# Instance normalisation over 512 instances: tiles of 64 KiB per partition in three slots in place of 32 KiB in six, with the squares shared by two engines and the last slot in three pieces

## The chip, the cores and the metric

The kernel runs on one core of a Trainium2 chip; the other cores are idle. The metric is the device time of one execution in microseconds (us). A profile's span is about 1.7 us shorter than the timed value of the same execution.

A run is called fast or slow: slow when it is over 1.5% above the fastest of the same kernel. On one core this is only a label by time. Ratios are the mean time of one kernel's fast runs over that of the other's fast runs of the same rounds, so not quite the ratio of the medians that are quoted.

PE is TensorE, DVE is VectorE, ACT is ScalarE, SP the engine that issues the loads. "ACTq" and "SPq" lines of a profile are the issues of transfers by ACT and SP.

## The reference, cut to what matters

```python
x = randn(8, 64, 32, 64, 64)              # float32, 512 instances of 131,072 elements, 268 MB
mean = np.mean(x, axis=(2, 3, 4), keepdims=True)
var = np.var(x, axis=(2, 3, 4), keepdims=True)
return ((x - mean) / np.sqrt(var + eps)).astype(np.float32)
```

Every byte is read once and written once: 536.87 MB through the core's 16 DMA engines.

## The kernel before

An instance is spread over 16 partitions of 8,192 columns, so a tile holds 8 instances and there are 64 tiles. Six slots of 32 KiB per partition hold tiles that are loading, computing or storing.

```python
    SPLIT = 16
    IPT = P // SPLIT
    F = n_elem // SPLIT          # 8192
    SLOTS = 6
    # ... data_pool = tile_pool(name="data", bufs=SLOTS)
    def load(g):
        t = data_pool.tile([P, F], fp32, name="xt")
        nc.sync.dma_start(out=t, in_=x_t[g])
        return t

    def compute(t):
        cut = F // 2
        # DVE sums t[:, :cut], ACT sums t[:, cut:]  -> sums [P, 2]
        # PE: matmul with a block matrix of 1/n_elem -> mean on every partition; DVE: neg_mean
        nc.scalar.activation(
            out=unused, in_=t, func=Act.Square, bias=neg_mean, accum_out=squares
        )
        # PE: matmul -> variance; ACT: sqrt; DVE: reciprocal (scale), neg_mean * scale (bias)
        # DVE normalises t[:, cut:], ACT normalises t[:, :cut], both in place

    with tc.manual_schedule():
        for g in range(n_tiles):
            t = load(g)
            compute(t)
            nc.scalar.dma_start(out=out_t[g], in_=t)
```

Of the kernel before, what the change touches and what calls it, by code (L numbers as in the profile page):

```python
# [1 line left out]

# [4 lines left out]


@with_exitstack
def kernel(  # L10
    ctx: ExitStack,
    tc: tile.TileContext,
    x: bass.AP,
    eps: bass.AP,
    out: bass.AP,
):
    nc = tc.nc
    fp32 = mybir.dt.float32
    Alu = mybir.AluOpType
    Act = mybir.ActivationFunctionType  # L20

    P = 128
    B, C, D, H, W = x.shape
    n_inst = B * C
    n_elem = D * H * W
    eps_f = float(eps)

    SPLIT = 16
    IPT = P // SPLIT
    F = n_elem // SPLIT  # L30
    n_tiles = n_inst // IPT
    SLOTS = 6

    x_t = x.rearrange("b c d h w -> (b c) (d h w)").rearrange(
        "(k i) (s f) -> k (i s) f", i=IPT, s=SPLIT
    )
    out_t = out.rearrange("b c d h w -> (b c) (d h w)").rearrange(
        "(k i) (s f) -> k (i s) f", i=IPT, s=SPLIT
    )

    singles = ctx.enter_context(tc.tile_pool(name="singles", bufs=1))
    data_pool = ctx.enter_context(tc.tile_pool(name="data", bufs=SLOTS))
    stat_pool = ctx.enter_context(tc.tile_pool(name="stats", bufs=4))
    psum_pool = ctx.enter_context(
        tc.tile_pool(name="psum", bufs=2, space=bass.MemoryType.PSUM)
    )


    avg = singles.tile([P, P], fp32, name="avg")
    nc.vector.memset(avg, 1.0 / n_elem)  # L50
    nc.gpsimd.affine_select(  # L51
        out=avg,
        in_=avg,
        pattern=[[-SPLIT, IPT], [0, SPLIT]],
        compare_op=Alu.is_ge,
        fill=0.0,
        base=0,
        channel_multiplier=1,
    )
    nc.gpsimd.affine_select(  # L60
        out=avg,
        in_=avg,
        pattern=[[SPLIT, IPT], [0, SPLIT]],
        compare_op=Alu.is_ge,
        fill=0.0,
        base=SPLIT - 1,
        channel_multiplier=-1,
    )

    eps_t = singles.tile([P, 1], fp32, name="eps_t")  # L70
    nc.vector.memset(eps_t, eps_f)  # L71

    unused = singles.tile([P, F], mybir.dt.uint8, name="unused")

    def load(g):
        t = data_pool.tile([P, F], fp32, name="xt")
        nc.sync.dma_start(out=t, in_=x_t[g])
        return t

    def compute(t):  # L80
        cut = F // 2
        sums = stat_pool.tile([P, 2], fp32, name="sums")
        nc.vector.reduce_sum(  # L83
            out=sums[:, 0:1], in_=t[:, :cut], axis=mybir.AxisListType.X
        )
        nc.scalar.activation(  # L86
            out=unused[:, cut:],
            in_=t[:, cut:],
            func=Act.Identity,
            accum_out=sums[:, 1:2],  # L90
        )
        mean_ps = psum_pool.tile([P, 2], fp32, name="mean_ps")
        nc.tensor.matmul(out=mean_ps, lhsT=avg, rhs=sums, start=True, stop=True)  # L93
        neg_mean = stat_pool.tile([P, 1], fp32, name="neg_mean")
        nc.vector.tensor_reduce(  # L95
            out=neg_mean,
            in_=mean_ps,
            axis=mybir.AxisListType.X,
            op=Alu.add,
            negate=True,  # L100
        )
        squares = stat_pool.tile([P, 1], fp32, name="squares")
        nc.scalar.activation(  # L103
            out=unused, in_=t, func=Act.Square, bias=neg_mean, accum_out=squares
        )
        var_ps = psum_pool.tile([P, 1], fp32, name="var_ps")
        nc.tensor.matmul(out=var_ps, lhsT=avg, rhs=squares, start=True, stop=True)  # L107
        std = stat_pool.tile([P, 1], fp32, name="std")
        nc.scalar.activation(out=std, in_=var_ps, func=Act.Sqrt, bias=eps_t)  # L109
        scale = stat_pool.tile([P, 1], fp32, name="scale")  # L110
        nc.vector.reciprocal(out=scale, in_=std)  # L111
        bias = stat_pool.tile([P, 1], fp32, name="bias")
        nc.vector.tensor_mul(out=bias, in0=neg_mean, in1=scale)  # L113
        nc.vector.tensor_scalar(  # L114
            out=t[:, cut:],
            in0=t[:, cut:],
            scalar1=scale,
            scalar2=bias,
            op0=Alu.mult,
            op1=Alu.add,  # L120
        )
        nc.scalar.activation(  # L122
            out=t[:, :cut], in_=t[:, :cut], func=Act.Identity, scale=scale, bias=bias
        )


    with tc.manual_schedule():
        for g in range(n_tiles):
            t = load(g)
            compute(t)  # L130
            nc.scalar.dma_start(out=out_t[g], in_=t)  # L131


# [1 line left out]
_INS = ['x', 'eps']  # L135
_OUTS = [((8, 64, 32, 64, 64), 'float32')]

_NUMBERS = {'eps': 9.999999747378752e-06}


# [26 lines left out]
```

## Time and profile before

| what | value | view |
|---|---|---|
| time | 1249.34 us median of 3 (1249.26 to 1250.57) | timed runs |
| span | 1247.6 us | page |
| busy: ACT, DVE | 961.6 us (77%), 467.4 us (37%) | page, part 1 |
| DMA | 9 or more tenths in 39 of 40 slices, mean 430 GB/s | page, part 2 |
| a data packet | 32,768 bytes, median 1,213 ns | packet records of the trace |
| one tile: DMA, compute | 19.4 us (8.39 MB in and out at 432 GB/s), 17.5 us | windows, timeline |

The page of the kernel before; the PE line gives the busy time of each engine, in the DMA row a digit is the busy share of one fortieth of the span in tenths, and the queue lines give packets, megabytes and the share of the 16 engines' span:

```profile
span 1247.6 us, 1828 instructions
...
PE 73.6 (6%) x256; PEld 64.2 (5%) x256; DVE 467.4 (37%) x322; ACT 961.6 (77%) x386; POOL 0.9 (0%) x6
...
DMA  9999999999999999999999999999999999999998
GB/s 403 420 437 434 434 427 436 435 435 427 435 436 434 434 428 435 435 434 427 437 435 434 433 429 437 435 432 427 437 436 434 429 431 435 436 434 425 437 436 364
DMA packets 18443, 536.99 MB, mean 430 GB/s; under 512 B 2048, under 2 KB 2048, under 8 KB 2048
...
q1 hardware_dynamic: 9216, 268.44, 49.9%
q10 hardware_dynamic: 9216, 268.44, 49.8%
```

The two queues (q1 loads, q10 stores) together keep the engines busy for 99.7% of the span. What is not at the full rate are the first slice (the first packet comes late) and the last one. The end, in windows of 5 us (the last two columns are the DMA's busy share and its rate):

```profile
1225.00:1230.00 5.00, 0.59 (x2) 0.50 (x2) 1.02 (x3) 3.85 (x4) 0.00 (x0) 1.00 0.99 426
1230.00:1235.00 5.00, 0.00 (x0) 0.00 (x0) 1.71 (x1) 3.15 (x1) 0.00 (x0) 1.00 0.81 347
1235.00:1240.00 5.00, 0.00 (x0) 0.00 (x0) 0.00 (x0) 0.00 (x0) 0.00 (x0) 1.00 0.98 419
```

At 1230 to 1235 us the rate falls to 347 GB/s: the store before the last has drained while ACT and DVE still normalise the last tile.

### The profile page before, as it was taken

Reading aid. Unit: us, or ns where it says so; the run is one execution under the profiler, and the core shown is the slowest. Engines: PE = TensorE matmul, PEld = TensorE weight load, DVE = VectorE, ACT = ScalarE, POOL = GpSimd, SP = SyncE. Lnnn points to the kernel's source line nnn. Section 1 sums busy time; section 2 is a strip of 40 time slices with the busy share of each in tenths; the row PEclk is TensorE's granted clock in tenths of the full one; section 3 lists DMA queues with packets and bytes.
Section 4 is the critical chain, followed back from the end, with each engine's and each line's share of the span. In section 5 each row is a group of like instructions: output and inputs, shape, how many; then the busy total and the mean of one; then the engine's idle time right before and its main releaser. Section 6 shows DMA issues by size and latency. Waiting matters only on the chain.

```text
span 1247.6 us, 1828 instructions
## 1 busy us (share of the span) xinstructions
PE 73.6 (6%) x256; PEld 64.2 (5%) x256; DVE 467.4 (37%) x322; ACT 961.6 (77%) x386; POOL 0.9 (0%) x6
## 2 busy tenths in 40 slices
PE   0000000000000000000000000000000000000000
PEld 0000000000000000000000000000000000000000
DVE  2344433433334334343343433434334333343331
ACT  5888888787777877778777777777787777877774
POOL 0000000000000000000000000000000000000000
DMA  9999999999999999999999999999999999999998
GB/s 403 420 437 434 434 427 436 435 435 427 435 436 434 434 428 435 435 434 427 437 435 434 433 429 437 435 432 427 437 436 434 429 431 435 436 434 425 437 436 364
DMA packets 18443, 536.99 MB, mean 430 GB/s; under 512 B 2048, under 2 KB 2048, under 8 KB 2048
## 3 DMA queue, kind: packets, MB, share of 16 engines
q1 hardware_dynamic: 9216, 268.44, 49.9%
q10 hardware_dynamic: 9216, 268.44, 49.8%
q14 instruction: 9, 0.07, 0.0%
q8 instruction: 2, 0.03, 0.0%
HBM read 268.44 MB, written 268.44 MB: 430 GB/s over the span
## 4 chain that ended last, share of the span: by engine, by line
ACT 45%; DVE 32%; another core or an unknown queue 12%; PE 6%; issue 2%; DMA 1%; ACTq 0%
ACT unused L103 37%; DVE sums L83 19%; DVE xt L114 10%; ACT xt L122 4%; ACT unused L86 3%; PE var_ps L107 3%; PE mean_ps L93 3%; ACT std L109 1%; DMA xt<-in_x_dram 1%; DVE scale L111 1%; DVE neg_mean L95 1%; DVE bias L113 1%; ACTq L131 0%; ACT L109 0%
## 5 line engine op out<-in xcount | busy, mean ns | idle before, releaser
L103 ACT ACTIVATE unused<-xt,neg_mean 128x8192 uint8<-128x8192 f32 x64 | 455.8, 7121 | 100.6 <-DVE neg_mean L95 100.6
L83 DVE TENSOR_REDUCE sums<-xt 128x1 f32<-128x4096 f32 x64 | 282.8, 4419 | 167.6 <-DMA xt<-in_x_dram 167.6
L86 ACT ACTIVATE unused<-xt 128x4096 uint8<-128x4096 f32 x64 | 231.5, 3617 | 96.1 <-DMA xt<-in_x_dram 91.5
L122 ACT ACTIVATE xt<-xt,bias,scale 128x4096 f32<-128x4096 f32 x64 | 243.3, 3801 | 31.3 <-DVE bias L113 31.3
L111 DVE RECIPROCAL scale<-std 128x1 f32<-128x1 f32 x64 | 10.5, 164 | 530.8 <-ACT std L109 530.8
L114 DVE TENSOR_SCALAR xt<-xt,scale,bias 128x4096 f32<-128x4096 f32 x64 | 154.4, 2413 | 2.7 <-DVE bias L113 0.3
L93 PE MATMUL mean_ps<-sums,avg 128*128 128x2 f32 x128 | 36.0, 351 | 670.9 <-DVE sums L83 573.9
L93 PEld LDWEIGHTS mean_ps<-sums,avg 128*128 128x128 f32 x128 | 32.1, 311 | 674.7 <-ACT unused L86 657.1
L107 PE MATMUL var_ps<-squares,avg 128*128 128x1 f32 x128 | 37.6, 363 | 484.1 <-ACT unused L103 484.1
L107 PEld LDWEIGHTS var_ps<-squares,avg 128*128 128x128 f32 x128 | 32.1, 312 | 489.6 <-ACT unused L103 489.6
L109 ACT ACTIVATE std<-var_ps,eps_t 128x1 f32<-128x1 f32 x64 | 16.7, 261 | 42.7 <-PE var_ps L107 42.7
L95 DVE TENSOR_REDUCE neg_mean<-mean_ps 128x1 f32<-128x2 f32 x64 | 10.2, 160 | 60.1 <-PE mean_ps L93 60.1
L103 ACT ACTIVATION_READ_ACCUMULATOR unused<-xt,neg_mean 128x1 f32 x64 | 11.9, 187 | 0.0
L86 ACT ACTIVATION_READ_ACCUMULATOR unused<-xt 128x1 f32 x64 | 11.9, 186 | 0.0
L113 DVE TENSOR_TENSOR bias<-neg_mean,scale 128x1 f32<-128x1 f32 x64 | 10.2, 160 | 2.2
L86 ACT ACT_TABLE_LOAD x1 | 1.3, 1283 | 0.8 <-PEq L148 0.8
L109 ACT ACT_TABLE_LOAD x1 | 1.3, 1283 | 0.0
L50 DVE MEMSET avg<- 128x128 f32 x1 | 0.2, 165 | 0.9 <-PEq L148 0.9
L51 POOL TENSOR_SCALAR_AFFINE_SELECT avg<-avg 128x128 f32<-128x128 f32 x1 | 0.3, 343 | 0.6 <-DVE eps_t L71 0.6
L60 POOL TENSOR_SCALAR_AFFINE_SELECT avg<-avg 128x128 f32<-128x128 f32 x1 | 0.3, 338 | 0.1
L148 POOL MEMSET const-bfloat16-1.0<- 128x1 bf16 x1 | 0.1, 102 | 0.0
L148 POOL MEMSET const-uint8-127<- 128x1 uint8 x1 | 0.1, 102 | 0.0
(3 smaller groups left out, 0.3 us busy)
## 6 DMA issues: line engine op xcount, KB each, us to landing
xt<-in_x_dram SPq DMA_DIRECT2D x64, 4096.0 KB, 53.3
out_dram<-xt ACTq DMA_DIRECT2D x64, 4096.0 KB, 45.2
```

The source lines that it names most:

```text
L51: nc.gpsimd.affine_select(out=avg, in_=avg, pattern=[[-SPLIT, IPT], [0, SPLIT]], compare_op=Alu.is_ge, fill=0.0, base=0, channel_multiplier=1,
L83: nc.vector.reduce_sum(out=sums[:, 0:1], in_=t[:, :cut], axis=mybir.AxisListType.X)
L86: nc.scalar.activation(out=unused[:, cut:], in_=t[:, cut:], func=Act.Identity, accum_out=sums[:, 1:2],)
L93: nc.tensor.matmul(out=mean_ps, lhsT=avg, rhs=sums, start=True, stop=True)
L95: nc.vector.tensor_reduce(out=neg_mean, in_=mean_ps, axis=mybir.AxisListType.X, op=Alu.add, negate=True,)
L103: nc.scalar.activation(out=unused, in_=t, func=Act.Square, bias=neg_mean, accum_out=squares)
L107: nc.tensor.matmul(out=var_ps, lhsT=avg, rhs=squares, start=True, stop=True)
L109: nc.scalar.activation(out=std, in_=var_ps, func=Act.Sqrt, bias=eps_t)
L111: nc.vector.reciprocal(out=scale, in_=std)
L113: nc.vector.tensor_mul(out=bias, in0=neg_mean, in1=scale)
L114: nc.vector.tensor_scalar(out=t[:, cut:], in0=t[:, cut:], scalar1=scale, scalar2=bias, op0=Alu.mult, op1=Alu.add,)
L122: nc.scalar.activation(out=t[:, :cut], in_=t[:, :cut], func=Act.Identity, scale=scale, bias=bias)
```

## The change

Its intent: fewer and larger transfers (32 in place of 64 tiles), the compute of a tile shortened by giving DVE a share of the squares, and a short end, because the last slot is loaded, computed and stored as three pieces of 8, 4 and 4 instances. The share of DVE needs scratch, which goes to PSUM, and its columns stay centred in place. The mean matrix carries the minus sign. The core of the diff (the averaging matrices for three row splits and unchanged calls are cut):

```diff
-    SLOTS = 6
+    SLOTS = 3
+    COLS = 16384
+    BIG = P * COLS // n_elem                 # 16 instances
+    tail = [
+        (n_inst - BIG, BIG // 2),
+        (n_inst - BIG // 2, BIG // 4),
+        (n_inst - BIG // 4, BIG // 4),
+    ]
 ...
-        cut = F // 2
+        a = w * 29 // 64                     # DVE sums [:a], ACT sums [a:]
+        b = w * 3 // 16                      # DVE squares [:b], ACT squares [b:]
+        c = w * 39 // 64                     # DVE normalises [:c], ACT [c:]
 ...
         nc.scalar.activation(
-            out=unused, in_=t, func=Act.Square, bias=neg_mean, accum_out=squares
-        )
+            out=of_act[:, : w - b], in_=t[:, b:], func=Act.Square,
+            bias=neg_mean, accum_out=squares[:, 1:2],
+        )
+        nc.vector.tensor_scalar(
+            out=t[:, :b], in0=t[:, :b], scalar1=neg_mean, scalar2=None, op0=Alu.add
+        )
+        nc.vector.tensor_tensor_reduce(
+            out=of_dve[:, :b], in0=t[:, :b], in1=t[:, :b], scale=1.0, scalar=0.0,
+            op0=Alu.mult, op1=Alu.add, accum_out=squares[:, 0:1],
+        )
 ...
-        for g in range(n_tiles):
-            t = load(g)
-            compute(t)
-            nc.scalar.dma_start(out=out_t[g], in_=t)
+        for g in range(n_big):
+            load(whole(g), *groups[g])
+            compute(tiles[g], groups[g][1])
+            store(tiles[g], *groups[g])
+        last = list(pieces(whole(n_big)))
+        for t, first, n in last:
+            load(t, first, n)
+        for t, first, n in last:
+            compute(t, n)
+            store(t, first, n)
```

Loads on SP and stores on ACT: the kernel before had this already.

More of the change, by code (lines that the diff above doesn't have):

```diff
@@ L26 @@
     eps_f = float(eps)
-    SPLIT = 16
-    IPT = P // SPLIT
-    F = n_elem // SPLIT
-    n_tiles = n_inst // IPT
-    SLOTS = 6
-    x_t = x.rearrange("b c d h w -> (b c) (d h w)").rearrange(
-        "(k i) (s f) -> k (i s) f", i=IPT, s=SPLIT
-    )
-    out_t = out.rearrange("b c d h w -> (b c) (d h w)").rearrange(
-        "(k i) (s f) -> k (i s) f", i=IPT, s=SPLIT
-    )
+    SLOTS = 3
+    COLS = 16384
+    x_f = x.rearrange("b c d h w -> (b c) (d h w)")
+    out_f = out.rearrange("b c d h w -> (b c) (d h w)")
@@ L41 @@
+    BIG = P * COLS // n_elem
+    groups = [(i, BIG) for i in range(0, n_inst - BIG, BIG)]
+    n_big = len(groups)
+    tail = [
[3 more added lines that the diff above has]
+    ]
     singles = ctx.enter_context(tc.tile_pool(name="singles", bufs=1))
     data_pool = ctx.enter_context(tc.tile_pool(name="data", bufs=SLOTS))
-    stat_pool = ctx.enter_context(tc.tile_pool(name="stats", bufs=4))
+    stat_pool = ctx.enter_context(tc.tile_pool(name="stats", bufs=3))
@@ L44 @@
+    psum_one = ctx.enter_context(
+        tc.tile_pool(name="psum_one", bufs=1, space=bass.MemoryType.PSUM)
+    )
     psum_pool = ctx.enter_context(
-        tc.tile_pool(name="psum", bufs=2, space=bass.MemoryType.PSUM)
+        tc.tile_pool(name="psum", bufs=1, space=bass.MemoryType.PSUM)
     )
-    avg = singles.tile([P, P], fp32, name="avg")
-    nc.vector.memset(avg, 1.0 / n_elem)
-    nc.gpsimd.affine_select(
-        out=avg,
-        in_=avg,
-        pattern=[[-SPLIT, IPT], [0, SPLIT]],
-        compare_op=Alu.is_ge,
-        fill=0.0,
-        base=0,
-        channel_multiplier=1,
-    )
@@ L60, with averaging @@
-    nc.gpsimd.affine_select(
-        out=avg,
-        in_=avg,
-        pattern=[[SPLIT, IPT], [0, SPLIT]],
-        compare_op=Alu.is_ge,
-        fill=0.0,
-        base=SPLIT - 1,
-        channel_multiplier=-1,
-    )
+    def averaging(split):
+        neg = singles.tile([P, P], fp32, name=f"neg{split}")
+        nc.vector.memset(neg, -1.0 / n_elem)
+        nc.gpsimd.affine_select(
+            out=neg,
+            in_=neg,
+            pattern=[[-split, P // split], [0, split]],
+            compare_op=Alu.is_ge,
+            fill=0.0,
+            base=0,
+            channel_multiplier=1,
+        )
+        nc.gpsimd.affine_select(
+            out=neg,
+            in_=neg,
+            pattern=[[split, P // split], [0, split]],
+            compare_op=Alu.is_ge,
+            fill=0.0,
+            base=split - 1,
+            channel_multiplier=-1,
+        )
+        return neg
@@ L70 @@
+    negs = {n: averaging(P // n) for n in sorted({n for _, n in groups + tail})}
     eps_t = singles.tile([P, 1], fp32, name="eps_t")
     nc.vector.memset(eps_t, eps_f)
-    unused = singles.tile([P, F], mybir.dt.uint8, name="unused")
-    def load(g):
-        t = data_pool.tile([P, F], fp32, name="xt")
-        nc.sync.dma_start(out=t, in_=x_t[g])
-        return t
-    def compute(t):
-        cut = F // 2
+    of_act = singles.tile([P, COLS - COLS * 3 // 16], mybir.dt.uint8, name="of_act")
@@ L82, in compute, with rows, load @@
+    of_dve = psum_one.tile([P, COLS * 3 // 16], fp32, name="of_dve")
+    def rows(ap, first, n):
+        return ap[first : first + n].rearrange("i (s f) -> (i s) f", s=P // n)
+    def load(t, first, n):
+        nc.sync.dma_start(out=t, in_=rows(x_f, first, n))
+    def compute(t, n):
+        w = t.shape[1]
+        a = w * 29 // 64
+        b = w * 3 // 16
+        c = w * 39 // 64
+        neg = negs[n]
         sums = stat_pool.tile([P, 2], fp32, name="sums")
         nc.vector.reduce_sum(
-            out=sums[:, 0:1], in_=t[:, :cut], axis=mybir.AxisListType.X
+            out=sums[:, 0:1], in_=t[:, :a], axis=mybir.AxisListType.X
@@ L85, in compute @@
         )
         nc.scalar.activation(
-            out=unused[:, cut:],
-            in_=t[:, cut:],
+            out=of_act[:, : w - a],
+            in_=t[:, a:],
             func=Act.Identity,
@@ L91, in compute @@
         )
-        mean_ps = psum_pool.tile([P, 2], fp32, name="mean_ps")
-        nc.tensor.matmul(out=mean_ps, lhsT=avg, rhs=sums, start=True, stop=True)
+        halves = psum_pool.tile([P, 2], fp32, name="halves")
+        nc.tensor.matmul(out=halves, lhsT=neg, rhs=sums, start=True, stop=True)
         neg_mean = stat_pool.tile([P, 1], fp32, name="neg_mean")
-        nc.vector.tensor_reduce(
-            out=neg_mean,
-            in_=mean_ps,
-            axis=mybir.AxisListType.X,
-            op=Alu.add,
-            negate=True,
-        )
-        squares = stat_pool.tile([P, 1], fp32, name="squares")
+        nc.vector.reduce_sum(out=neg_mean, in_=halves, axis=mybir.AxisListType.X)
+        squares = stat_pool.tile([P, 2], fp32, name="squares")
+        nc.scalar.activation(
+            out=of_act[:, : w - b],
+            in_=t[:, b:],
+            func=Act.Square,
+            bias=neg_mean,
+            accum_out=squares[:, 1:2],
+        )
+        nc.vector.tensor_scalar(
+            out=t[:, :b],
+            in0=t[:, :b],
+            scalar1=neg_mean,
+            scalar2=None,
+            op0=Alu.add,
+        )
+        nc.vector.tensor_tensor_reduce(
+            out=of_dve[:, :b],
+            in0=t[:, :b],
+            in1=t[:, :b],
+            scale=1.0,
+            scalar=0.0,
+            op0=Alu.mult,
+            op1=Alu.add,
+            accum_out=squares[:, 0:1],
+        )
+        neg_var = psum_pool.tile([P, 1], fp32, name="neg_var")
+        nc.tensor.matmul(
+            out=neg_var, lhsT=neg, rhs=squares[:, 0:1], start=True, stop=False
+        )
+        nc.tensor.matmul(
+            out=neg_var, lhsT=neg, rhs=squares[:, 1:2], start=False, stop=True
+        )
+        std = stat_pool.tile([P, 1], fp32, name="std")
         nc.scalar.activation(
-            out=unused, in_=t, func=Act.Square, bias=neg_mean, accum_out=squares
+            out=std, in_=neg_var, func=Act.Sqrt, scale=-1.0, bias=eps_t
         )
-        var_ps = psum_pool.tile([P, 1], fp32, name="var_ps")
-        nc.tensor.matmul(out=var_ps, lhsT=avg, rhs=squares, start=True, stop=True)
-        std = stat_pool.tile([P, 1], fp32, name="std")
-        nc.scalar.activation(out=std, in_=var_ps, func=Act.Sqrt, bias=eps_t)
         scale = stat_pool.tile([P, 1], fp32, name="scale")
@@ L113, in compute @@
         nc.vector.tensor_mul(out=bias, in0=neg_mean, in1=scale)
+        nc.scalar.activation(
+            out=t[:, c:], in_=t[:, c:], func=Act.Identity, scale=scale, bias=bias
+        )
         nc.vector.tensor_scalar(
-            out=t[:, cut:],
-            in0=t[:, cut:],
+            out=t[:, b:c],
+            in0=t[:, b:c],
             scalar1=scale,
@@ L121, in compute, with whole, pieces, store @@
         )
-        nc.scalar.activation(
-            out=t[:, :cut], in_=t[:, :cut], func=Act.Identity, scale=scale, bias=bias
-        )
-    with tc.manual_schedule():
-        for g in range(n_tiles):
-            t = load(g)
-            compute(t)
-            nc.scalar.dma_start(out=out_t[g], in_=t)
+        nc.vector.tensor_scalar(
+            out=t[:, :b], in0=t[:, :b], scalar1=scale, scalar2=None, op0=Alu.mult
+        )
+    tiles = {}
+    def whole(g):
+        tiles[g] = data_pool.tile([P, COLS], fp32, name="xt")
+        return tiles[g]
+    def pieces(t):
+        at = 0
+        for first, n in tail:
+            width = n * n_elem // P
+            yield t[:, at : at + width], first, n
+            at += width
+    def store(t, first, n):
+        nc.scalar.dma_start(out=rows(out_f, first, n), in_=t)
+    with tc.manual_schedule():
+        for g in range(n_big):
[8 more added lines that the diff above has]
+            store(t, first, n)
 _INS = ['x', 'eps']
```

## The prediction

> **What bounds it now.** The 16 DMA engines. The page's DMA row is 9 in 39 of 40 slices, and the queue table gives 49.9% + 49.8% = 99.7% of the engines' span; 536.99 MB moved at a mean 430 GB/s. The trace's own packet records show how: 16,384 data packets of 32,768 bytes, nearly all taking 1,213 ns, plus 2,048 completion writes of 4 bytes at 9 ns. Per engine that is 1,024 x 1.213 + 128 x 0.009 = 1,243.3 us of the 1,247.6 us span. 32,768 B / 1.213 us x 16 = 432 GB/s, and the steady windows read 432. The Trainium skill (DMA: Bandwidth & Descriptors, "Where 436 GB/s comes from") puts the ceiling at 435.2 GB/s; the trace is 0.7% under it. ACT (77% busy) and DVE (37%) wait for data: DVE's first reduction waits 167.6 us in all for loads.
>
> **What is left to win.** About 1.2 us before the first packet, about 1.3 us at 1,232-1,234 us where the store before last has drained and the last tile is still being normalised, and some 3 us from the last full-rate stretch to the end (stragglers, completion).
>
> **What the change does.**
> 1. Bytes: the same 536.87 MB. Queues as before. No gain.
> 2. Rows of 64 KiB, 32 + 32 big transfers for 64 + 64: completion writes fall by about 0.6 us per engine. If a row becomes one 64 KiB packet, and if the 8 ns of 1,213 above the ceiling's 1,205 is a cost per packet, another 512 x 8 ns = 4 us go; if it is a cost per byte, or rows are cut into 32 KiB, nothing. I count half: -2 us.
> 3. Compute per 16,384-column tile, estimated from the trace's durations (ACT 0.86 ns per column plus 0.3 us, DVE sum 1.04, in-place scale 0.55-0.59): sums 8.0, mean 1.0, squares 11.7 (ACT; DVE's share about 5), variance to scale 1.4, normalise 5.9: 28.5 us, against 2 x 17.5 = 35 us now. DMA needs 38.8 us per such tile. All off the critical path: no gain.
> 4. Three slots: load 38.8 + compute 28.5 + store 38.8, plus about 4 us of receipts and issue, is 110 of 3 x 38.8 = 116 us. It fits, with 6 us to spare: steady DMA stays full, one load and one store in flight.
> 5. Head: the first load lands at about 23 us, tile 0 is stored from 52, tile 1 from 81. The three loads and store 0 are done at about 80: one bubble of about 2 us.
> 6. Tail: when the last piece lands, store 30 (8 MB, 19 us) still drains; the pieces' compute (15.5, 9, 9 us) hides behind it. The 1.3 us bubble goes.
>
> Sum: 1249.3 - 0.6 - 2 + 2 - 1.3 = **1247.4 us**, range 1241.5 to 1255. Within 2%: 0.97; faster by over 2%: 0.01 (it would beat the fabric ceiling); slower: 0.02.
>
> **What would show it.** Data packets of 64 KiB and their duration (2.418 us for a per-packet cost, 2.426 for per-byte); DMA still 9 everywhere; ACT near 62% busy and DVE near 48%; ACT's wait for the load about 10 us per tile; the dip near 80 us; no dip before the last store; last slice above 364 GB/s.
>
> **What would make it wrong.** The three-slot loop not closing: compute above about 34 us per tile (the fused square-and-sum on DVE has no record in this trace), or gaps when only one load is outstanding; then each of 32 tiles loses microseconds. Longer row pitch slowing HBM. Or the engines drifting apart more, with longer stragglers at the end.

## The result, and the profile after

| | runs (us) | median | fast runs |
|---|---|---|---|
| before | 4 runs, 1249.26 to 1250.57 | 1249.3 | all |
| after | 1250.58, 1253.14, 1276.28, 1277.63 | 1264.71 | 1250.58 and 1253.14 |

The ratio of the fast runs is 1.0018 (95% interval 0.9994 to 1.0042): the same within 2%. But two of four runs took 2% longer, and the kernel before has no such runs. The profile was taken on the run of 1250.58 us. Its page:

```profile
span 1248.9 us, 1271 instructions
...
PE 58.9 (5%) x204; PEld 51.1 (4%) x204; DVE 618.3 (50%) x310; ACT 812.5 (65%) x206; POOL 2.1 (0%) x10
...
DMA  9999999999999999999999999999999999999997
GB/s 403 437 437 428 418 428 435 433 437 437 437 435 437 432 432 432 424 437 437 435 435 432 437 436 435 435 437 435 432 435 424 435 431 437 430 437 437 429 436 330
DMA packets 9800, 536.95 MB, mean 430 GB/s; under 512 B 1088, under 2 KB 1088, under 8 KB 1088
...
q1 hardware_dynamic: 4896, 268.44, 49.9%
q10 hardware_dynamic: 4896, 268.44, 49.6%
```

How long ACT waited for loads in all, how often, and the longest wait (view of the waits):

```profile
ACT of_act L103 <- DMA xt<-in_x_dram: 349.3, 30, 20.6
```

There are half as many packets. The middle is full, there is no dip near 80 us (slice 3 reads 437), and the last slice is lower than before: 330 in place of 364 GB/s. The end of the changed kernel in windows of 5 us:

```profile
1225.00:1230.00 5.00, 0.00 (x0) 0.00 (x0) 0.00 (x0) 0.00 (x0) 0.00 (x0) 1.00 0.95 410
1230.00:1235.00 5.00, 0.57 (x2) 0.50 (x2) 3.27 (x4) 3.16 (x3) 0.00 (x0) 1.00 1.01 433
1235.00:1240.00 5.00, 1.17 (x4) 1.00 (x4) 2.42 (x6) 3.84 (x4) 0.00 (x0) 1.00 0.45 193
```

The hole at the end did not go; it grew, to 45% busy over 5 us. Its timeline (start, duration, engine, line) names the reason:

```profile
1224.17 0.34 ACTq L184 DMA_DIRECT2D out_dram<-xt  x1
1230.91 2.07 ACT L103 ACTIVATE of_act<-xt 128x2240 uint8<-128x2240 f32 x1 [6.77 <-DMA xt<-in_x_dram]
...
1240.34 0.34 ACTq L184 DMA_DIRECT2D out_dram<-xt  x1
```

ACT was ready for the last piece at 1224 us but waited 6.77 us for its load, which landed 63.6 us after its issue; only then could the last 9.4 us of compute start.

### Where the microseconds of the fast run went

The packet records allow a balance. Each record is one packet on one engine; where an engine's packets are chained, the next starts 4 ns before the one before it ends, so records overlap a little. From the first to the last packet, per engine (sum of all records over 16, less the overlap, plus the time in which an engine ran no packet):

| us per engine | before | after | difference |
|---|---|---|---|
| data packets at their nominal time | 1242.1 | 1238.3 | -3.8 |
| overlap of the records | -4.1 | -2.3 | +1.8 |
| packets beyond nominal ("excess") | 1.9 | 4.1 | +2.2 |
| completion writes | 1.2 | 0.6 | -0.6 |
| no packet running | 3.4 | 4.9 | +1.5 |
| first to last packet | 1244.5 | 1245.6 | +1.1 |

Nominal are the usual times: 2,418 ns for 65,536 bytes, 1,213 for 32,768, 611 for 16,384. Thus 64 KiB rows are one packet, and one of them costs 4 ns less than two of 32 KiB once the overlap is counted; the gain of the larger tiles is 2.6 us (-3.8 + 1.8 - 0.6), and the fast run gives it back as longer packets and as idle engines at the end.

### The profile page after: what moved, and what is told of

Its sections match the earlier page's. It is cut to its first block, busy times and chain, and to the rows that moved or that the text cites. A ratio compares the mean times of both kernels' runs of the same rounds, so it can differ in the third digit from the quotient of the medians.

```text
span 1248.9 us, 1271 instructions
## 1 busy us (share of the span) xinstructions
PE 58.9 (5%) x204; PEld 51.1 (4%) x204; DVE 618.3 (50%) x310; ACT 812.5 (65%) x206; POOL 2.1 (0%) x10
## 4 chain that ended last, share of the span: by engine, by line
DMA 71%; ACT 18%; DVE 8%; PE 1%; issue 1%; another core or an unknown queue 1%; ACTq 0%; SPq 0%
DMA xt<-in_x_dram 37%; DMA out_dram<-xt 35%; ACT of_act L115 11%; DVE sums L100 7%; ACT xt L155 6%; ACT of_act L103 1%; PE halves L110 1%; PE neg_var L143 1%; ACT std L148 0%; DVE scale L152 0%; DVE bias L154 0%; DVE neg_mean L112 0%; ACT L148 0%; ACTq L184 0%
## 5 line engine op out<-in xcount | busy, mean ns | idle before, releaser
L103 ACT ACTIVATE of_act<-xt 128x8960 uint8<-128x8960 f32 (+2 forms) x34 | 245.8, 7231 | 351.0 <-DMA xt<-in_x_dram 349.3
L100 DVE TENSOR_REDUCE sums<-xt 128x1 f32<-128x7424 f32 (+2 forms) x34 | 252.6, 7430 | 354.9 <-DMA xt<-in_x_dram 354.9
L115 ACT ACTIVATE of_act<-xt,neg_mean 128x13312 uint8<-128x13312 f32 (+2 forms) x34 | 365.0, 10736 | 37.2 <-DVE neg_mean L112 37.2
L155 ACT ACTIVATE xt<-xt,bias,scale 128x6400 f32<-128x6400 f32 (+2 forms) x34 | 183.9, 5408 | 16.5 <-DVE bias L154 16.5
L158 DVE TENSOR_SCALAR xt<-xt,scale,bias 128x6912 f32<-128x6912 f32 (+2 forms) x34 | 124.7, 3668 | 1.3
L129 DVE CUSTOM_DVE_ANT_0 of_dve<-xt 128x3072 f32<-128x3072 f32 (+2 forms) x34 | 108.1, 3180 | 1.2
L122 DVE TENSOR_SCALAR xt<-xt,neg_mean 128x3072 f32<-128x3072 f32 (+2 forms) x34 | 58.7, 1726 | 1.2
L166 DVE TENSOR_SCALAR xt<-xt,scale 128x3072 f32<-128x3072 f32 (+2 forms) x34 | 58.5, 1721 | 0.0
L143 PE MATMUL neg_var<-squares,neg 128*128 128x1 f32 x68 | 19.9, 362 | 180.3 <-ACT of_act L115 180.3
L140 PE MATMUL neg_var<-squares,neg 128*128 128x1 f32 x68 | 19.9, 362 | 179.7 <-DVE squares L129 179.7
L143 PEld LDWEIGHTS neg_var<-squares,neg 128*128 128x128 f32 x68 | 17.0, 311 | 183.2 <-ACT of_act L115 183.2
L140 PEld LDWEIGHTS neg_var<-squares,neg 128*128 128x128 f32 x68 | 17.0, 311 | 182.7 <-DVE squares L129 182.7
L112 DVE TENSOR_REDUCE neg_mean<-halves 128x1 f32<-128x2 f32 x34 | 5.4, 160 | 27.5 <-PE halves L110 27.5
```

What stands on the lines that cost most here:

```text
L100: nc.vector.reduce_sum(out=sums[:, 0:1], in_=t[:, :a], axis=mybir.AxisListType.X)
L103: nc.scalar.activation(out=of_act[:, : w - a], in_=t[:, a:], func=Act.Identity, accum_out=sums[:, 1:2],)
L115: nc.scalar.activation(out=of_act[:, : w - b], in_=t[:, b:], func=Act.Square, bias=neg_mean, accum_out=squares[:, 1:2],)
L122: nc.vector.tensor_scalar(out=t[:, :b], in0=t[:, :b], scalar1=neg_mean, scalar2=None, op0=Alu.add,)
L129: nc.vector.tensor_tensor_reduce(out=of_dve[:, :b], in0=t[:, :b], in1=t[:, :b], scale=1.0, scalar=0.0, op0=Alu.mult, op1=Alu.add, accum_ou ...
L140: nc.tensor.matmul(out=neg_var, lhsT=neg, rhs=squares[:, 0:1], start=True, stop=False)
```

## The experiments

Two questions were open: where do the runs of 1253 to 1278 us come from, and why did the three pieces not close the hole at the end of the fast run? The theories have names in the expectations: LOOP (the tight loop of slots leaves the DMA engines idle), PACKET (the packets themselves get longer), SIZE (packets of 64 KiB are at fault), COLD (explained with runs 1 and 2) and SHARE (beside long packets, short ones get the smaller share of an engine). "Excess" is the quantity of the table above. The "lead" of a store is the time from the end of its issue on ACT to the start of its first packet (median over the 16 engines); stores are numbered from 0. The trace does not name the engine of a packet. For the balance I rebuilt it by chaining each packet to the one that ended when it began; a few labels swap that way (an engine gets about 540 to 548 of 544 packets). The first packets of a store of 64 KiB rows need no labels: they are the 16 of its 128 that start first, within 5 us of each other.

### 1, 2. The changed kernel again, to catch a long run

No edit.

> The changed kernel unaltered, for one more look: two of its four runs took 1276 to 1278 us and left no trace. A look of about 1250 us should show the trace already seen: 64 KiB packets of 2.418 us, an idle DMA only in the last 15 us. A look of about 1277 us should tell two theories apart. Theory LOOP (three slots leave about 6 us of slack per tile, so a small disturbance opens gaps): the packets keep 2.42 us and the 16 DMA engines stand idle for about 25 us more in all than the 4.9 us of the fast trace. Theory PACKET (long rows meet the memory badly in some runs): the engines stay full and the packets' own time grows by some 25 us per engine.

> As for the run before, the changed kernel unaltered: a second chance to catch a long run (two of four were long). LOOP: idle engines, packets unchanged. PACKET: longer packets, engines full.

Measured: 1255.66 and 1270.48 us, state unknown, one look each. The second is a long run with a trace. Its page against the changed kernel's fast page above: the DMA row is full all the same, but the rate sags to 401 to 411 GB/s in six slices of the middle.

```profile
span 1268.8 us, 1271 instructions
...
DMA  9999999999999999999999999999999999999998
GB/s 417 409 430 430 430 434 432 434 430 432 434 401 428 432 430 430 407 426 430 426 430 428 430 402 430 430 424 403 428 426 426 407 430 419 411 446 428 437 429 348
```

Idle engines account for nothing of it (4.0 us, against 4.9 in the fast trace); the excess of the packets is 24.8 us per engine, against 4.1. So LOOP in its first form (engines standing idle) falls, and the lost time is inside packets, as PACKET said. The excess is not spread evenly over them, however. In the worst trace (run 8 below), 250 of the 307 store packets that took over 20% too long were the first of the eight that an engine moves for a store, and, after the first 80 us, about 120 of 133 for loads. The timeline shows what is special about them. These are the issues of a store (ACTq) and of the next load (SPq). The load of a slot is issued as soon as the store from that slot has landed, so the SPq line also marks when the previous store was over. First the fast run, then the long one:

```profile
812.05 0.34 ACTq L184 DMA_DIRECT2D out_dram<-xt  x1
818.25 0.33 SPq L90 DMA_DIRECT2D xt<-in_x_dram  x1
850.70 0.34 ACTq L184 DMA_DIRECT2D out_dram<-xt  x1
856.84 0.33 SPq L90 DMA_DIRECT2D xt<-in_x_dram  x1
```

```profile
826.46 0.34 ACTq L184 DMA_DIRECT2D out_dram<-xt  x1
829.59 0.33 SPq L90 DMA_DIRECT2D xt<-in_x_dram  x1
866.78 0.34 ACTq L184 DMA_DIRECT2D out_dram<-xt  x1
869.18 0.33 SPq L90 DMA_DIRECT2D xt<-in_x_dram  x1
```

In the fast run a store is issued 6.1 to 6.2 us before the previous one has landed, in the long run 2.4 to 3.1 us. From the packet records, store by store in order (lead in us, and how much longer than nominal the first packets took, mean of the engines, in us; stores 3 to 14):

```
fast run   lead    7.4  5.2  5.2  4.2  4.1  4.1  4.1  4.0  4.1  4.2  4.1  4.1
           excess 0.00 0.00 0.00 0.00 0.00 0.00 0.00 0.00 0.00 0.00 0.00 0.00
long run   lead    5.1  4.8  4.0  3.2  2.2  1.3  2.0  1.0  2.0  1.1  2.1  1.4
           excess 0.00 0.00 0.00 0.05 0.34 0.66 0.48 0.67 0.44 0.72 0.51 0.73
```

The lead of the long run shrinks store by store to about 2 us, and once it is under about 2.5 us the first packets of every store shown take 0.3 to 0.7 us longer on the mean of the engines. In the fast run it falls to about 4 us and stays there to the end. I call this theory COLD: a store that reaches its queue late pays in its first packet.

### 3. Half the tile in six slots

```diff
-    SLOTS = 3
-    COLS = 16384
+    SLOTS = 6
+    COLS = 8192
```

> The changed kernel with 8,192 columns in six slots in place of 16,384 in three: same memory, same division of the work between the engines, same tail scheme at half the size, 32 KiB packets. If 64 KiB packets are worth the 8 ns per packet, the steady part pays about 4 us per engine more than the changed kernel (packets of 1.213 us). Both theories of the long runs say that they go: all runs within 0.3%, as with the kernel before; if long runs stay, both are wrong and the compute part is the suspect. Time 1247 to 1251 us.

Measured: 1257.34 to 1261.74 us in four runs, ratio 1.0079 (1.0062 to 1.0096). No run stands out (0.35% from end to end, 0.3% expected), but the time is above the expected range. Only 6.3 us is excess; 11.1 us is idle, 10.1 us of it in the last 40 us. The cause of that is found in run 12: one store near the end waits 24 us for a completion semaphore.

### 4. The last whole tile's store cut in four

```diff
-    def store(t, first, n):
-        nc.scalar.dma_start(out=rows(out_f, first, n), in_=t)
+    def store(t, first, n, cut=1):
+        whole_rows = rows(out_f, first, n)
+        w = t.shape[1] // cut
+        for j in range(cut):
+            nc.scalar.dma_start(
+                out=whole_rows[:, j * w : (j + 1) * w], in_=t[:, j * w : (j + 1) * w]
+            )
 ...
-            store(tiles[g], *groups[g])
+            store(tiles[g], *groups[g], cut=4 if g == n_big - 1 else 1)
```

> The changed kernel with only the store of the last whole tile cut in four, so that its packets are 16 KiB like those of the last two loads. In the fast trace the last loads (16 KiB packets) crawl at 12 to 39 GB/s beside that store (64 KiB packets, about 410 GB/s) from 1205 to 1230 us, and the DMA is nearly idle at 1237 to 1241 us. Theory SHARE (each engine alternates packet by packet between the two queues, so the shorter packets get the smaller share): the last load lands 10 us or more earlier (before 1221 us), the hole closes, and a fast run gains 2 to 4 us. Rival (the hole is the compute of the last piece, whatever its load does): the last store is still issued at about 1240 us and the time stays. The long runs should be as many as before.

Measured: 1251.72, 1264.5, 1275.69, 1276.63 us; two of the four are long, as with the changed kernel. The trace is of the run of 1264.5 us. In the changed kernel, an engine that still has load packets when the big store starts sends one 16 KiB load packet for each 64 KiB store packet: their starts are 3.0 us apart (2.41 + 0.61), where they were 0.61 us apart with the queue alone. With the store cut, they are 1.2 us apart. The last load lands 48.6 us after its issue in place of 63.6, no piece waits for its load any more, and the DMA stays full up to the last store:

```profile
1240.00:1245.00 5.00, 1.12 (x4) 1.00 (x4) 3.01 (x5) 4.07 (x3) 0.00 (x0) 1.00 1.02 439
1245.00:1250.00 5.00, 0.64 (x3) 0.50 (x2) 2.03 (x4) 2.93 (x4) 0.00 (x0) 1.00 0.95 406
1250.00:1255.00 5.00, 0.00 (x0) 0.00 (x0) 0.00 (x0) 0.00 (x0) 0.00 (x0) 1.00 0.99 419
1255.00:1260.00 5.00, 0.00 (x0) 0.00 (x0) 0.00 (x0) 0.00 (x0) 0.00 (x0) 1.00 0.13 56
```

This supports SHARE: the turns are seen packet by packet, and both traces with the cut store (this one and run 11) have no wait for the last load. It is not the whole cause, though: of the uncut traces the changed kernel's fast run and runs 1 and 10 have the wait (6.8, 8.0 and 8.6 us), but run 2, also uncut, has none, and its DMA is 0.89 busy or more in windows of 5 us up to 1260 us. What decides between the two is not shown. The cut gained nothing that the times could show: the best run (1251.72 us) is no better than the changed kernel's, and in the trace one engine ends its last store 6.5 us after most of the others (the 56 GB/s of the last line), so 6.4 us stay idle. The Trainium skill ("DMA: Bandwidth & Descriptors", section "Queues, rings and completion order") says that an engine takes turns between queue rows packet by packet; the 3.0 us and 1.2 us agree.

This trace also shows COLD switching on and off within one run. Its stores 6 to 19 are in the state of the long runs with leads of 0.6 to 2.8 us; at store 20 the lead jumps to 4.9 us, stays above 3.3, and the excess is 0.00 from there on.

### 5. 32 KiB packets in the changed kernel's slots

```diff
+    def move(engine, dst, src):
+        for at in range(0, dst.shape[1], COLS // 2):
+            end = min(at + COLS // 2, dst.shape[1])
+            engine.dma_start(out=dst[:, at:end], in_=src[:, at:end])
 ...  load and store call move (shortened)
```

> The changed kernel with every whole-tile transfer cut in two column halves: 32 KiB packets, but the same three slots of 64 KiB, the same compute, and the same rows. Theory SIZE (long packets are what goes wrong with 64 KiB packets): the time of a packet goes back to 1.213 us with under 1 us per engine of excess in the steady part, all runs agree within 0.5%, at about 1253 us (4 us per engine for twice the packets). Rival LOOP (the three-slot loop lets a queue run dry at every tile, so the engines lose the even load-store alternation and get into bad relative positions): excess of 5 us per engine or more stays in the long runs and the runs still spread by over 1%.

Measured: six runs of 1250.15 to 1254.61 us, median 1250.87, ratio 1.0013 (1.0000 to 1.0027); excess 3.6 us. SIZE's expectation holds (its time was 2 us too high): of the excess, 3.1 us falls in the first 100 us and 0.4 us in the steady part. Runs 7 and 8 below, with 64 KiB packets on the same chip, were long. But the cut also loosens the loop: SP issues the load of half a slot when that half has been stored, so this run alone does not separate packet size from queueing. In the steady part no store had a lead under 3.4 us.

### 6. The kernel before with four slots

```diff
-    SLOTS = 6
+    SLOTS = 4
```

> The kernel before with four slots of 32 KiB in place of six, nothing else. The loop of a slot is load 19.4, compute 17.5, store 19.4 and about 4 us of receipts, 60 of 4 x 19.4 = 78 us, so the DMA can stay full. LOOP: with fewer transfers queued a queue can run dry more often; packets with neighbours of the same direction appear, and the excess of packet time grows from 0.4 to several us per engine: 1252 to 1265 us with a spread. SIZE: packets are as short as before, so the time stays at 1249 to 1250 us with all runs within 0.2%.

Measured: 1251.6, 1252.56, 1252.65 and 1260.13 us, ratio 1.0034 (1.0011 to 1.0058). By its times LOOP could be right (1252 to 1265 us with a spread were expected of it), and SIZE, with all runs within 0.2% at 1249 to 1250 us, is not. But the trace lacks what LOOP was to work by: the excess is 2.3 us (1.9 before), not several. The leads of the steady part are 6.4 us or more, so short leads with packets of 32 KiB were not tried here either. The trace of the run of 1251.6 us has 5.3 us idle, nearly all of it one hole at the end. Neither theory had that; the run of 1260 us left no trace. LOOP as stated is not supported by the trace, and the spread of the runs stays unexplained.

### 7. The old division of work in the new slots

```diff
-        a = w * 29 // 64
-        b = w * 3 // 16
-        c = w * 39 // 64
+        a = w // 2
+        c = w // 2
 ...  all squares on ACT, in two halves (a scratch of 16 KiB does not fit beside three slots)
```

> The changed kernel with the division of work of the kernel before: all squares on ScalarE, sums and normalisation split in halves; tiles, slots and tail as changed. Compute per tile rises from 27.6 us to an estimated 33 us (squares 14.4, sums 8.7, normalise 7.3, the rest 2.7). Reading of the prediction: the loop needs about 38.8 + 33 + 38.8 + 4 = 115 of 116 us, so it just closes in the steady part; the last pieces take some 20% longer. Time within 0.5% of the changed kernel's fast runs in the best run, at most 5 us more. Rival (the rebalanced compute is what keeps the DMA full): idle DMA of several us in the middle of the trace, 1265 us or more in every run.

Measured: 1267.49, 1268.93, 1290.39, 1299.51 us, ratio of the fast ones 1.0146 (1.0129 to 1.0164). The compute of a tile is 32.8 us, as estimated. My reading of the prediction (it just closes, no loss) falls; the rival's time (1265 us or more in every run) holds, but it named the wrong place, for the idle time in the whole of the trace before its last 40 us is 2.6 us. The loss is excess: 19.7 us. 20 of the 27 stores in the steady part have leads under 3 us. So the shared squares do matter in this loop: with 5 us more compute the median lead of these stores is 1.8 us in place of 4.1, and even the best run is long.

### 8. The last slot whole

```diff
-    tail = [(n_inst - BIG, BIG // 2), (n_inst - BIG // 2, BIG // 4), (n_inst - BIG // 4, BIG // 4)]
+    tail = [(n_inst - BIG, BIG)]
```

> The changed kernel with its last slot loaded, computed and stored whole. With equal packets on both queues the last load should land near 1209 us and not be starved, but its compute of 27.6 us is then in one piece: the store before it drains at about 1222 us, the last store starts at about 1237 us and takes 20 us: an idle DMA of about 15 us and a span of about 1258 us if the packets are short (more by the excess if they are long). If the pieces bought nothing, the span would be 1249 us.

Measured: 1291.65 us, one look, state unknown, and the longest excess of all: 29.9 us, 25 of 27 steady stores with leads under 3 us. The end can be read apart from that. From 1255 us to 1265 us the DMA does nothing at all while the last tile is computed:

```profile
1250.00:1255.00 5.00, 0.00 (x0) 0.00 (x0) 4.92 (x3) 5.00 (x1) 0.00 (x0) 1.00 0.07 30
1255.00:1260.00 5.00, 0.58 (x2) 0.50 (x2) 0.00 (x0) 5.00 (x1) 0.00 (x0) 1.00 0.00 0
1260.00:1265.00 5.00, 0.59 (x2) 0.50 (x2) 2.74 (x3) 3.85 (x4) 0.00 (x0) 1.00 0.00 0
```

18.5 us are idle in the last 40 us (20.6 less 2.1), against 4.5 with the pieces: the pieces are worth about 14 us in this kernel, near the 15 expected.

### 9. 32 KiB packets, loop as tight as in the changed kernel

```diff
-        for at in range(0, w, step):
+        for at in reversed(starts) if backwards else starts:     # backwards for loads
 ...  shown against run 5, shortened
```

> The stable run with 32 KiB packets loosened the loop too: half a slot could be loaded as soon as that half was stored, and its stores waited 3.1 us or more in the queue. This kernel keeps the 32 KiB packets but loads the second half of a slot first, so that no load can be issued before the whole slot is stored, as in the changed kernel. Theory SIZE (64 KiB packets are the fault): first packets of a store keep 1.213 us whatever their lead, all runs within 0.5% of 1251 us. Theory COLD (a store's first packet takes about 0.8 us longer when it starts less than some 2.5 us after its issue, as in the long runs of the changed kernel: 0.8 to 1.0 of those packets there, none above 3 us): long runs come back, 1255 to 1280 us, and in a long run the first store packets with a lead under 2.5 us are the ones stretched.

Measured: 1250.05, 1250.22, 1250.27, 1250.47 us, ratio 1.0005 (0.9991 to 1.0020), excess 3.4 us. Long runs did not come back, as SIZE said and COLD did not. Yet COLD's rule was not put to the test: the smallest lead of a steady store (of its first half, which goes first) was 3.6 us. What differs is how the lead moves: it went from 4.6 us to 3.6 us over 25 tiles here, where the long run of the changed kernel lost 4 us within six stores.

### 10. Shorter compute

```diff
-            out=of_act[:, : w - b],
-            in_=t[:, b:],
+            out=of_act[:, : w // 4],
+            in_=t[:, w - w // 4 :],
             func=Act.Square,
```

> Wrong on purpose: ScalarE sums the squares of a quarter of the columns only, so the compute of a tile takes about 21 us in place of 27.6; slots, tiles, 64 KiB packets and tail as in the changed kernel. COLD: a store is issued some 6 us earlier, its first packet has a lead of 3 us or more in every tile, excess of packet time below 5 us per engine, and all runs lie within 0.5% near 1247 us; the wrong values change no time. SIZE: packets are as long as ever, the runs spread from 1250 to 1278 us as before.

Measured: 1255.92 to 1260.42 us in four runs, ratio 1.0069 (1.0056 to 1.0082), with the wrong values that were intended. The spread of the runs falls to 0.4%, as COLD said. The time does not fall to the 1247 us of the expectation, nor the excess below its 5 us (7.3 us), and the trace (the run of 1260.42 us) says why: 11.5 us idle, in the last 40 us, because the load of the last piece was starved again and landed at 1243 us. In the middle, the leads begin at 13.5 us in place of 7.4 and then shrink all the same, to 9.1 at store 12, 5.5 at store 17 and 2.6 at store 24; excess on the first packets appears from store 23 on. The expectation of "3 us or more in every tile" failed, but the rule held in the same trace (one store, 23, was lengthened by 0.16 us at a lead of 3.7 us).

### 11. One pass over the data

```diff
+        # ACT: squares of t without the mean, in two halves, and the sum of w // 12 columns
+        # DVE: the sum of the other columns; PE: one matmul of the four partial sums
+        nc.vector.tensor_scalar(out=neg_var, in0=neg_mean, scalar1=neg_mean,
+                                scalar2=neg_sq, op0=Alu.mult, op1=Alu.add)
 ...  shortened, in part in words: no centring, no DVE squares; the last whole store cut in four as in run 4
```

> Meant to beat both kernels, and right: sums and squares in one pass (variance as the mean of squares less the square of the mean), so the compute of a tile falls from 27.6 to an estimated 24 us, with the last whole tile's store cut in four as in the earlier run. COLD: the lead of the stores grows by about 3 us, few or no long runs, excess below 6 us per engine; with 64 KiB packets and no hole at the end a span of about 1246 us, 1247 to 1249 us timed. SIZE: long runs stay as frequent as in the changed kernel, 1250 to 1278 us.

Measured: 1248.88, 1249.19, 1249.19, 1249.79, 1252.02, 1255.86 us, median 1249.49; ratio 1.0009 (0.9994 to 1.0025). Right values. The compute of a tile is 23.7 us. In the trace (the run of 1252.02 us) no steady store has a lead under 3.4 us, and the excess is 3.2 us. It has no run as long as the changed kernel's, and three runs a little below the kernel before, but it does not beat it, and five of the six runs miss the 1247 to 1249 us expected: 7.3 us are idle, most of it one engine that ends its last store at 1249.4 us when the others are done by 1241 to 1247 us.

### 12. The kernel before with its last tile halved

```diff
-        for g in range(n_tiles):
+        for g in range(n_tiles - 1):
 ...
+        for t, first in halves:             # two pieces of 4 instances
+            nc.sync.dma_start(out=t, in_=rows(x_f, first))
+        for t, first in halves:
+            compute(t, avg_half)
+            nc.scalar.dma_start(out=rows(out_f, first), in_=t)
 ...  shortened: the second averaging matrix, rows and halves are left out
```

> The kernel before with one idea of the change alone, at its own sizes: the last tile is loaded, computed and stored as two halves (16 KiB rows), everything else as it was. In the trace of before the DMA dips at 1232 to 1234 us (1.3 us) because the last tile is stored only when all of it is normalised. If that hole is all the tail can give, it closes: the last store is issued about 1236 us but is only 2 MB, and the time falls by about 1.3 us to 1248.0 us with all runs as close together as before. If the shorter packets of the last loads (16 KiB beside 32 KiB) starve them as in the changed kernel (SHARE), the last load lands later than the 1215 us of before, near 1225 us, and half of the gain or more is lost: 1248.7 us or above. COLD: with six slots every store waits over 9 us in its queue, so no long runs.

Measured: 1256.86 to 1257.27 us in five runs, ratio 1.0062 (1.0048 to 1.0075): 7.8 us longer, and in every run. None of my expectations was that large. The timeline shows the loss far ahead of the piece:

```profile
1131.72 3.80 ACT L128 ACTIVATE xt<-xt,bias,scale 128x4096 f32<-128x4096 f32 x1 [0.48 <-DVE bias L119]
1137.06 4.42 DVE L89 TENSOR_REDUCE sums<-xt 128x1 f32<-128x4096 f32 x1 [2.99 <-DMA xt<-in_x_dram]
...
1156.52 0.34 ACTq L137 DMA_DIRECT2D out_dram<-xt  x1
1156.91 3.62 ACT L92 ACTIVATE unused<-xt 128x4096 uint8<-128x4096 f32 x1 [21.39 <-DMA xt<-in_x_dram]
```

ACT has normalised its half at 1135.5 us, and issues that store only at 1156.52 us. The profile books the wait to the load of the next tile, but DVE began on that tile at 1137.06 us. The trace's operands tell what ACT waits for: in these programs eight completion semaphores serve all transfers in turn, and this store waits for the one that it will itself signal (number 106), whose last user was the load of tile 60, landing at 1156.5 us:

```
store 58: issued 1156.8, semaphore 106; previous user load 60, landed 1156.7     (this kernel)
store 59: issued 1157.4, semaphore 106; previous user load 60, landed 1157.3     (the kernel before)
```

(The two rows are from the trace's records, with its clock 0.3 us ahead of the profile's.) In the kernel before, the same semaphore falls to the next store, which was ready at 1155.5 us and so waits about 1.5 us. One load more near the end moves the turn by one, and the wait becomes 21 us; ACT computes nothing during it, and the remaining tiles then follow without a pause and end late. The same stands in the trace of run 3 (on the profile's clock): ACT has normalised at 1160.7 us, but store 59 is issued only at 1184.3 us, when load 61, the previous user of its semaphore, has landed at 1184.2 us. This run therefore says nothing about SHARE in the kernel before; it shows a different cost of an added piece.

### The stores of all traces with 64 KiB packets together

Eight traces: after, runs 1, 2, 4, 7, 8, 10 and 11; stores 3 to 29 of each, 216 in all.

| lead of the store | stores | first packet longer by, mean | stores with over 0.1 us | first packet of the load beside it longer by, mean |
|---|---|---|---|---|
| under 1 us | 16 | 0.36 us | 12 | 0.88 us |
| 1 to 2 us | 46 | 0.68 us | 46 | 0.09 us |
| 2 to 2.5 us | 20 | 0.36 us | 20 | 0.03 us |
| 2.5 to 3 us | 20 | 0.08 us | 6 | 0.03 us |
| 3 us and more | 114 | 0.00 us | 1 | 0.03 us |

The load beside a store is the one into the slot that the store before has just left (stores 3 to 28 for this column; its first packets are again the 16 that start first). The four stores with a lead under 1 us that were hardly lengthened, by 0.04 to 0.10 us, are no exception: there the load beside them took 1.1 to 1.3 us longer. Store and load together lose more, the shorter the lead.

| trace | steady stores under 3 us lead (of 27) | excess, us per engine | span, us |
|---|---|---|---|
| after | 0 | 4.1 | 1248.9 |
| one pass (11) | 0 | 3.2 | 1250.3 |
| short compute (10) | 6 | 7.3 | 1258.7 |
| last store cut (4) | 14 | 16.6 | 1262.8 |
| again, first (1) | 14 | 8.0 | 1253.9 |
| longer compute (7) | 20 | 19.7 | 1267.2 |
| again, second (2) | 23 | 24.8 | 1268.8 |
| whole tail (8) | 25 | 29.9 | 1289.9 |

The first packets of stores and loads make up most of the excess: 11.8 and about 5 of 24.8 us in run 2, 13.2 and about 8 of 29.9 us in run 8.

## Why the prediction was right or wrong

The prediction called the time the same (1247.4 us, 1241.5 to 1255), and the fast runs (mean 1251.9 us, ratio 1.0018) are. The two long runs lie outside its range, and so does the median of all four.

1. **DMA bounds both kernels: right.** The DMA row is full in both, ACT and DVE wait. ACT's wait for loads is 349.3 us, 10.3 us for each of the 34 tiles and pieces (about 10 predicted); ACT is 65% and DVE 50% busy (62 and 48 predicted).
2. **Larger packets: right in sum, by luck in the parts.** The packets are 64 KiB and take 2.418 us, the per-packet value. I read that as 8 ns a packet and counted half of 4 us. The records overlap by 4 ns at each seam, so the true saving is 2.0 us: the counted sum, not by the counted reason.
3. **Compute 28.5 us per tile: right.** Measured 27.5 us, from the reduction at 629.57 us to the store's issue at 657.10 us.
4. **"It fits, with 6 us to spare: steady DMA stays full": this step failed.** The slack was there (a lead of 5 to 7 us at the start in the traces of this kernel), and the engines did stay full, but the slack is not kept: the lead falls in all eight 64 KiB traces. In the fast run it stops at about 4 us and costs nothing. In the long ones it falls below 2.5 us, and there a store and the load beside it together lose 0.4 to 1.2 us per engine in their first packets (means of the groups above). The excess is then 3 to 26 us above the 4.1 us of the fast run. The prediction's list of what could go wrong had the loop not closing with idle gaps; the loss came without a visible gap, as longer packets.
5. **A bubble of 2 us near 80 us: wrong.** The second store was issued at 78.6 us, before the queues were dry; the engines were idle for at most 0.01 us from 60 to 100 us.
6. **The tail's bubble goes: wrong.** The pieces are worth about 14 us in this kernel (run 8), but the hole grew from 1.3 us to some 3 us, because I let the last load land while the store before was draining. On the engines that still had some, its 16 KiB packets got one turn per 64 KiB store packet (run 4), so it landed late; run 2 shows that it is not late enough to leave a hole in every run. The last slice read 330 and not above 364 GB/s.

What stays open. Why a late store's first packet takes longer is not shown: at the head of the run the second store starts 0.7 to 2.3 us after its issue with nothing added, and the one 32 KiB store with a lead of 0.6 us (run 3) was not lengthened either. So a short lead seems to mark the state in which both queues turn to a new transfer at once; it may not be enough by itself. Why the lead shrinks is not shown either. In the traces where first packets are not lengthened, the start of a load against the store beside it moves mostly in steps of about one packet of 2.4 us (4.8 and 7.1 us in the fast run, 4.8, 7.2 and 9.5 us in run 11), and with 32 KiB packets it stayed at 4.9 us (run 9, but for two tiles). This fits SIZE, and ten executions with 32 KiB packets in three slots (runs 5 and 9) had no time above 1254.6 us, but the step was not forced on purpose. Short leads with 32 KiB packets never came about in the steady part, so SIZE and COLD are not separated: both may be needed. The runs of 1276 to 1278 us themselves left no trace; the ones read are of 1264 to 1292 us. The chip is a rival that was not tested: runs 5 to 8 were on another chip than runs 1 to 4, runs 9 to 11 on a third, and the unaltered changed kernel was not run on those, so part of the absence of long runs in runs 5, 9, 10 and 11 could be the chip's. Runs 7 and 8 were long on the second chip, and run 10 shows lengthened first packets on the third. No version tried beats the kernel before.

## What to carry to other kernels

When a kernel already moves its bytes at the full rate, a larger tile can win only what a packet and a completion cost, here 2.6 of 1249 us, and it spends the queue's depth for it: keep stores issued some microseconds before their queue runs dry (3 us or more cost nothing here), and look at the spread of several runs, not at one profile. Next to long packets, short ones starved here (one per 3.0 us in place of 0.61): give the last loads the same packet length as the stores that run beside them. After adding a transfer, look at every issue that comes late and at the semaphore it waits for; a wait booked to a load can be the reuse of a completion semaphore.

## What the Trainium skill lacked or had wrong

- "DMA: Bandwidth & Descriptors", "Where 436 GB/s comes from": the ceiling of 435 GB/s is right to 1% (432 GB/s in steady windows). The warning there, that for transfers between HBM and SBUF a limit of about 358 GB/s on the HBM side binds, does not hold for this core running alone: 536.87 MB between the two moved at a mean of 430 GB/s.
- No page has durations for rows of this length: a 64 KiB row is one packet of 2,418 ns, 32 KiB take 1,213 ns and 16 KiB 611 ns.
- The same page, "Queues, rings and completion order": taking turns packet by packet agrees, but the page does not draw the consequence for unequal packets: 16 KiB beside 64 KiB gets one packet per 3.0 us, beside 16 KiB one per 1.2 us.
- No page has the lengthened first packet: 78 of the 82 stores with a lead under 2.5 us had first packets over 0.1 us longer (up to 0.86 us, mean of the engines), 1 of the 114 with 3 us or more; at the other four the load beside was lengthened.
- No page says that a program may use its completion semaphores in turn (eight here) and that the issue of a transfer then waits for an older, unrelated one: 21 us on ACT in run 12, 24 us in run 3.
